# Three one-element vector steps written another way, and rows loaded one tile ahead, in a two-layer mixer kernel

## The chip, the cores and the metric

The kernel runs on one core of a Trainium2 chip. The core has a matrix engine (TensorE, PE in the rows; PEld is its weight load), a vector engine (VectorE, DVE), a scalar engine (ScalarE, ACT), GpSimd (POOL) and SyncE (SP), whose queue issues every DMA of this kernel. Each engine runs its own list of instructions in order and waits for others by semaphores. On-chip memory is SBUF, and PSUM for what the matrix engine writes. The metric is the device time of one execution in microseconds (us).

## The reference

Two layers over a sequence of 1024 rows of width 1024; 16 heads of 64. Layer 0 is a causal attention with a forget gate, layer 1 a sliding-window attention at three dilations.

```python
def rms_norm(x, g):
    xf = x.astype(jnp.float32)
    y = xf * lax.rsqrt(jnp.mean(xf * xf, axis=-1, keepdims=True) + EPS) * g.astype(jnp.float32)
    return y.astype(x.dtype)

def reference(x, positions, norm_g, ...):
    cos, sin = rotary_tables(positions)
    for i in range(DEPTH):                      # DEPTH = 2
        h = rms_norm(x, norm_g[i])
        if i % N_MIXERS == 0:
            o, gate = fox_mixer(h, ...)
        else:
            o, gate = dsw_mixer(h, cos, sin, ...)
        x = x + (o * jax.nn.silu(gate)) @ w_out
    return x
```

The factor 1/sqrt(mean(x²)+eps) of a row is what the change's first part computes. It is needed once for each of the 1024 rows at either layer's input: eight tiles of 128 rows, one row a partition.

## The kernel before

Activations live transposed in SBUF as two parts that sum to the float32 value, `xh` and `xl`, 8 blocks of 128 features by 1024 rows. `project` (L305) multiplies one tile of 128 rows by a slab of weights: for each of the 8 blocks three matmuls (xh·w, xh·w_low, xl·w), 24 in all, into one PSUM tile `pj`. Three `pj` buffers exist; the transposes of `transpose_rows` (`pt`, L322) take theirs from the same three. Where a `pj` has not been read out, the matmuls of a later tile wait.

Weights arrive as `raw` tiles by DMA (`load`, L245, two buffers) and are split into a high part on ScalarE (L286) and a low part on GpSimd or, for some blocks, VectorE (L288).

The program has one order of emission, with a clock of slots (`Flow`): each two blocks of a projection tick it, and work put down for a slot is emitted there. A scheduler of the framework then sets the order of the instructions on VectorE, ScalarE, GpSimd and the DMA queue by its own estimate of durations; TensorE's order is pinned to that of the program.

The change touches two stretches:

- *The first gate part of layer 0 (0 to about 57 us).* `gates` (L463) projects 8 tiles; in front of each, `x_ready` (L570) loads and splits a later tile of x (L525, L528, L530, L531; VectorE or GpSimd multiply and subtract) and calls `row_factor` (L539): a sum of squares on ScalarE (L542), two small steps (L543, L544), `inv_sqrt` (L330 to L336) and a negation (L546). The gate value of tile t takes L475 on VectorE, then L476, L477 and L478 on ScalarE, then L482 on VectorE, which reads `pj` for the last time. `load_gbc` (L359 to L361) and `gain_tables` (L157 to L172) also stand in this stretch.
- *The last part of layer 0's out projection (about 620 to 680 us; `h == 2` in the loop at L761).* For each of 8 tiles: load `xr` (the input rows, three buffers of tag `n2k`) and `xf` (two halves of the rows written by the parts before, seven buffers of tag `ga`), project, add (L780), store (L781), then `norm_rows` (L341): squares on ScalarE (L345), a sum (L347), a scale (L348), `inv_sqrt`, and two products `xn` (L352), stored by L784 and later transposed (L324, copies L327 on ScalarE and L328 on VectorE) into `xh` and `xl`.

`inv_sqrt` takes y = exp(-0.5 ln v) on ScalarE and one Newton step y(1.5 - 0.5 v y²) on VectorE, on tiles of 128 x 1. It is called 8 times in each of the two stretches and nowhere else.

Of the kernel before, what the change touches and what calls it, by code (L numbers as in the profile page):

```python
# [17 lines left out]
ALU = mybir.AluOpType  # L18
# [4 lines left out]
P = 128  # L23
# [3 lines left out]
NT = S // P  # L27
# [24 lines left out]
def tile_cols(g, t):  # L52


    if g < 2:
        return slice(t * P, (t + 1) * P, 1)
    a = 2 * P * (t % 4) + t // 4
    return slice(a, a + 2 * 127 + 1, 2)
# [24 lines left out]
def trunk(ctx, tc, ins, out, cfg):  # L83
    nc = tc.nc
# [31 lines left out]
    def lay(shape, dtype, name, tag):  # L116
        return layer["pool"].tile(shape, dtype, name=name, tag=tag, bufs=layer["bufs"][tag])
# [4 lines left out]
    x1_d = dram.tile([S, D], F32, name="x1_d")  # L122
# [112 lines left out]
    class Weights:  # L235
# [9 lines left out]
        def load(self, i, tag=None):  # L245
            if tag is None:
                self.raw[i] = w_p.tile([P, 2, 384], F32, name="raw", tag="raw", bufs=2)
            else:
                self.raw[i] = lay([P, 2, 384], F32, name="raw", tag=tag)
            nc.sync.dma_start(self.raw[i][:, :, : self.n], self.src[:, 2 * i : 2 * i + 2, :])  # L250
# [51 lines left out]
    def part(src, i, layer=0):  # L302
        return Weights(src[i], src[i].shape[2], None, layer)

    def project(w, cols, last=None):  # L305

        n = w.n
        ps = under["ps"] = ps_pj.tile([P, 512], F32, name="pj", tag="pj")
        for k in range(KT):
            assert k < KT - 2 or last is None or last in turned  # L310
            for i, (a, j) in enumerate(((xh, 0), (xh, 1), (xl, 0))):
                nc.tensor.matmul(ps[:, :n], a[:, k, cols], w.slabs[k][:, j, :n], start=(k == 0 and i == 0), stop=(k == KT - 1 and i == 2))  # L312
            if k % 2:
                flow.tick()
        return ps


    def transpose_half(row, h, t, own=False):
        transpose_rows(row, 4 * h, 4, t, own)
# [10 lines left out]
    def inv_sqrt(y, v, n, a):  # L330

        nc.scalar.activation(y, v, AF.Ln)
        nc.scalar.activation(y, y, AF.Exp, scale=-0.5)
        nc.vector.tensor_mul(a, y, y)
        nc.vector.scalar_tensor_tensor(a, a, -0.5, v, ALU.mult, ALU.mult)
        nc.vector.scalar_tensor_tensor(y, a, 1.5, y, ALU.add, ALU.mult)  # L336

    def rows2(name, tag="ga"):
        return [lay([P, 512], F32, name=f"{name}{h}", tag=tag) for h in range(2)]
# [15 lines left out]
    def load_gbc(layer):  # L355
        gbc = lay([P, D], F32, name="gbc", tag="ph")
        nc.sync.dma_start(gbc, norm_g[layer].partition_broadcast(P))
        gm = gmax[:, layer : layer + 1]
        nc.vector.tensor_reduce(gm, gbc, AX.X, ALU.max, apply_absolute_value=True)  # L359
        nc.vector.tensor_mul(gmax2[:, layer : layer + 1], gm, gm)  # L360
        nc.vector.tensor_scalar(gmax2[:, layer : layer + 1], gmax2[:, layer : layer + 1], 2.0 * D, None, ALU.mult)  # L361
        return gbc
# [365 lines left out]
    for hp in range(NHP):  # L728
# [11 lines left out]
        for t in range(NT):  # L740
# [13 lines left out]
            if hp == NHP - 1:  # L754

                a = max(flow.now + 6, s0 + cfg["due"][t] - 4 * NT + cfg["lpf"] + 9)
# [4 lines left out]
    for h, (c0, n) in enumerate(PARTS):  # L761
        w2 = (part(w_fo, h + 1) if h < 2 else part(w_gate, 0)).ahead()
        if h == 1:
            gbc2 = load_gbc(1)
            rotary_tables()
        for t in range(NT):
            rows = slice(t * P, (t + 1) * P)
            xr = sb.tile([P, n], F32, name="xr", tag="n2k", bufs=cfg["nb"])
            nc.sync.dma_start(xr, x[rows, c0 : c0 + n])
            if h == 2:  # L770
                xf = rows2("xf")
                nc.sync.dma_start(xf[0], x1_d[rows, :512])
                nc.sync.dma_start(xf[1][:, : c0 - 512], x1_d[rows, 512:c0])
            ps = project(w, tile_cols(0, t), t)
            if h < 2:
                xo = sb.tile([P, n], F32, name="xo", tag="n2k", bufs=cfg["nb"])
                nc.vector.tensor_add(xo, ps[:, :n], xr)
                nc.sync.dma_start(x1_d[rows, c0 : c0 + n], xo)
            else:
                nc.vector.tensor_add(xf[1][:, c0 - 512 :], ps[:, :n], xr)  # L780
                nc.sync.dma_start(x1_d[rows, c0:], xf[1][:, c0 - 512 :])  # L781
                xn = norm_rows(xf, gbc2)
                for i in range(2):
                    nc.sync.dma_start(xn_d[rows, i * 512 : (i + 1) * 512], xn[i])  # L784
                    flow.at(flow.now + cfg["lx"] + i, lambda xn=xn, i=i, t=t: transpose_half(xn[i], i, t))
        w = w2
# [185 lines left out]
    for h, (c0, n) in enumerate(PARTS):  # L972
        w2 = part(w_do, h + 1).ahead() if h < 2 else None
        for t in range(NT):
            rows = tile_rows(1, t)
            xr = sb.tile([P, n], F32, name="xr", tag="n2k", bufs=cfg["nb"])
# [59 lines left out]
```

## Time and profile before

| | us |
|---|---|
| time, median of 3 runs | 1816.96 |
| lowest and highest run | 1816.78, 1818.73 |
| the profiled execution | 1819.76 |
| its span, first to last instruction | 1818.0 |
| TensorE busy in the span | 1752.1 (96%) |
| VectorE, ScalarE, GpSimd busy | 1110.1, 985.4, 951.8 |

The profiled execution lies 2.80 us above the median of the timed runs, and 1.76 us of it lie outside the span. The mean granted clock was 0.995 of full speed.

In a row of the timeline the columns are: start in us, duration in us, engine, source line, operation, out<-in by the program's names, shape and type, a count where equal neighbours are merged, and in brackets how long the engine was idle before and what released it. A stretch row of the windows view gives, for each engine, busy us and (x instructions), then the granted clock, the DMA share and GB/s.

### The profile page before, as it was taken

How to read it: one execution, taken by the hardware profiler on the slowest of the kernel's cores; microseconds unless marked ns; L12 is line 12 of the kernel's file. 1: busy time of each engine (PE TensorE's matmuls, PEld its weight loads, DVE VectorE, ACT ScalarE, POOL GpSimd, SP SyncE). 2: the span in 40 equal slices, each digit the busy share in tenths (PEclk: the TensorE clock that was granted, in tenths of full speed). 3: DMA queues.
4: the chain of work that ended last, by engine and by line, in shares of the span. 5: the costliest groups of instructions: out<-in, count | busy, mean ns of one | idle time of the engine just before them, and what ended most of it. 6: DMA issues, size and time to landing. Idle time of an engine off the chain costs nothing.

```text
span 1818.0 us, 39235 instructions
## 1 busy us (share of the span) xinstructions
PE 1752.1 (96%) x13784; PEld 1686.9 (93%) x13784; DVE 1110.1 (61%) x3774; ACT 985.4 (54%) x2642; POOL 951.8 (52%) x1161
## 2 busy tenths in 40 slices
PE   7999999999989989999999999999999999999999
PEld 6999888888878989999999999999999999999899
DVE  8546666766665373365556576676676667767631
ACT  6536666666664354445555665555555555555610
POOL 4215665556653211255656656667576666757520
PEclk9999999999999999999999999999999999999999
DMA  7437999989998563456776696666776766667842
GB/s 287 123 117 137 186 200 184 174 178 183 193 202 198 167 206 113 121 108 140 134 141 144 146 203 132 152 141 152 141 154 151 169 142 142 155 137 189 194 138 93
DMA packets 630790, 289.28 MB, mean 159 GB/s; under 512 B 510384, under 2 KB 595376, under 8 KB 630592
## 3 DMA queue, kind: packets, MB, share of 16 engines
q1 hardware_dynamic: 630592, 286.77, 69.5%
q8 instruction: 108, 1.77, 0.4%
q14 instruction: 90, 0.74, 0.1%
HBM read 124.87 MB, written 37.03 MB: 89 GB/s over the span
## 4 chain that ended last, share of the span: by engine, by line
PE 53%; DMA 17%; DVE 12%; ACT 7%; POOL 5%; issue 4%; SPq 1%; DVEq 0%; POOLq 0%; ACTq 0%
PE pj L312 46%; DMA raw<-in_w_dsw 4%; DMA raw<-in_w_fox 3%; PE s L448 3%; DMA ptt<-ph 3%; POOL w L288 2%; DVE p L659 2%; POOL ph L499 2%; DMA qk_t<-hl 1%; ACT p L493 1%; POOL hl L423 1%; DMA x_d<-xo 1%; ACT ph L496 1%; PE pt L324 1%; ACT w L286 1%
## 5 line engine op out<-in xcount | busy, mean ns | idle before, releaser
L312 PE MATMUL pj<-w,xh 128*128 128x384 f32 (+2 forms) x5632 | 1443.4, 339 | 20.5 <-ACT w L286 6.2
L312 PEld LDWEIGHTS pj<-w,xh 128*128 128x128 f32 x5632 | 999.1, 190 | 30.6 <-ACT w L286 7.3
L312 PE MATMUL pj<-w,xl 128*128 128x384 f32 (+2 forms) x2816 | 939.7, 334 | 4.6 <-DVE xl L328 2.6
L312 PEld LDWEIGHTS pj<-w,xl 128*128 128x128 f32 x2816 | 535.5, 190 | 6.3 <-DVE xl L328 3.3
L288 POOL TENSOR_TENSOR w<-raw,w 128x384 fp32r<-128x384 f32 (+2 forms) x258 | 261.4, 1033 | 305.1 <-ACT w L286 300.1
L499 POOL TENSOR_TENSOR ph<-p,ph 128x512 f16<-128x512 f32 (+3 forms) x176 | 172.7, 998 | 161.5 <-ACT ph L496 138.3
L286 ACT CAST w<-raw 128x384 fp32r<-128x384 f32 (+2 forms) x352 | 162.2, 501 | 120.7 <-PE pj L312 51.9
L423 POOL TENSOR_TENSOR hl<-u,hl 128x512 f16<-128x512 f32 x128 | 150.8, 1178 | 132.0 <-ACT hl L422 132.0
L850 POOL TENSOR_TENSOR ph<-p,ph 128x768 f16<-128x768 f32 (+2 forms) x96 | 155.8, 1623 | 104.8 <-ACT ph L849 104.7
L378 ACT ACTIVATE sq<-pj 128x256 f32<-128x256 f32 x256 | 97.0, 379 | 194.0 <-DVE u L373 192.3
L448 PE MATMUL s<-qk_t 128*128 128x128 f16 (+1 forms) x1504 | 160.9, 247 | 8.5 <-DVE acc L659 6.2
L255 DVE TENSOR_REDUCE vm<-raw 128x1 f32<-128x256 f32 x128 | 53.6, 419 | 156.6 <-DMA raw<-in_w_dsw 111.5
L507 PEld LDWEIGHTS <-ptt 128*128 128x128 f16 x1136 | 103.5, 98 | 43.3 <-issue 24.2
L448 PEld LDWEIGHTS <-qk_t 128*128 128x128 f16 x1504 | 110.6, 98 | 24.6 <-issue 15.4
L493 ACT ACTIVATE p<-p,acc 128x512 f32<-128x512 f32 (+2 forms) x192 | 109.9, 610 | 39.6 <-DVE acc L659 35.5
L422 ACT CAST hl<-u 128x512 f16<-128x512 f32 x128 | 79.1, 618 | 91.4 <-DVE u L420 86.6
L496 ACT CAST ph<-p 128x512 f16<-128x512 f32 (+3 forms) x176 | 89.2, 536 | 60.8 <-DMA ptt<-ph 60.8
L391 DVE TENSOR_REDUCE pj<-sq 128x8 f32<-128x512 f32 x128 | 88.4, 691 | 46.3 <-ACT sq L378 46.2
L845 ACT ACTIVATE p<-p,og 128x128 f32<-128x128 f32 (+1 forms) x256 | 97.8, 441 | 32.6 <-DVE og L844 32.5
L373 DVE TENSOR_TENSOR u<-pj,gr 128x256 f32<-128x256 f32 x256 | 106.4, 416 | 12.4 <-PE pj L312 12.0
L424 DVE COPY hl<-hl 128x512 f16<-128x512 f16 x128 | 61.9, 483 | 78.6 <-POOL hl L423 78.5
L508 PEld LDWEIGHTS <-ptt 128*128 128x128 f16 x1136 | 106.3, 97 | 0.5 <-issue 0.5
(167 smaller groups left out, 2293.2 us busy)
## 6 DMA issues: line engine op xcount, KB each, us to landing
raw<-in_w_dsw SPq DMA_DIRECT2D x96, 384.0 KB, 3.7
raw<-in_w_fox SPq DMA_DIRECT2D x32, 384.0 KB, 3.9
og_d<-og SPq DMA_DIRECT2D x64, 132.0 KB, 2.9
cmb<-og_d SPq DMA_DIRECT2D x64, 132.0 KB, 3.3
bc<-c_d SPq DMA_DIRECT2D x32, 256.0 KB, 3.9
gs_d<-ge SPq DMA_DIRECT2D x32, 192.0 KB, 2.3
xt<-in_xt SPq DMA_DIRECT2D x16, 256.0 KB, 6.1
xrow<-in_x SPq DMA_DIRECT2D x8, 512.0 KB, 6.9
```

Of the source, the lines that this page charges most:

```text
L286: nc.scalar.copy(w[:, 0, :n], raw[:, k % 2, :n])
L288: eng.tensor_sub(w[:, 1, :n], raw[:, k % 2, :n], w[:, 0, :n].bitcast(F32))
L312: nc.tensor.matmul(ps[:, :n], a[:, k, cols], w.slabs[k][:, j, :n], start=(k == 0 and i == 0), stop=(k == KT - 1 and i == 2))
L373: nc.vector.tensor_mul(u[:, t % 2].rearrange("p (a b) d -> p a b d", a=2), ps[:, : 4 * HD].rearrange("p (a b d) -> p a b d", a=2, b=2), gr ...
L423: nc.gpsimd.tensor_sub(hl[:, :, :4, 1], u, hl[:, :, :4, 0])
L448: nc.tensor.matmul(s[:, c0 : c0 + cnt * P].rearrange("p (c s) -> p c s", c=cnt), qk[:, i, blk], kk[:, j : j + cnt, e], start=(h == 0), sto ...
L493: nc.scalar.activation(p, p, AF.Exp, bias=acc, scale=-1.0)
L496: nc.scalar.copy(ph[:, e, 0, cols], p)
L499: (nc.gpsimd if pool_l else nc.vector).tensor_sub(ph[:, e, 1, cols], p, ph[:, e, 0, cols])
L507: nc.tensor.matmul(o[:, e, :], hi, vt[:, j, e, HD:], start=(b == 0), stop=False, skip_group_check=True)
L508: nc.tensor.matmul(o[:, e, :HD], hi, vt[:, j, e, :HD], start=False, stop=False, skip_group_check=True)
L850: nc.gpsimd.tensor_sub(ph[:, 1], st["p"], ph[:, 0])
```

## The change

`inv_sqrt` computes the same Newton step in three instructions that take one tensor and one or two scalars (numbers, or one value a partition) instead of a product of two tensors and two instructions of the form (tensor, scalar, tensor). In the out projection the loads of a tile are put into a function, and in the last part those of tile t+1 are emitted ahead of the projection of tile t.

```diff
         nc.scalar.activation(y, v, AF.Ln)
         nc.scalar.activation(y, y, AF.Exp, scale=-0.5)
-        nc.vector.tensor_mul(a, y, y)
-        nc.vector.scalar_tensor_tensor(a, a, -0.5, v, ALU.mult, ALU.mult)
-        nc.vector.scalar_tensor_tensor(y, a, 1.5, y, ALU.add, ALU.mult)
+        nc.vector.tensor_scalar(a, y, y, -0.5, ALU.mult, ALU.mult)
+        nc.vector.tensor_scalar(a, a, v, 1.5, ALU.mult, ALU.add)
+        nc.vector.tensor_scalar(y, y, a, None, ALU.mult)
...
-        for t in range(NT):
+        def load(t):
             rows = slice(t * P, (t + 1) * P)
             xr = sb.tile([P, n], F32, name="xr", tag="n2k", bufs=cfg["nb"])
             nc.sync.dma_start(xr, x[rows, c0 : c0 + n])
-            if h == 2:
-                xf = rows2("xf")
-                nc.sync.dma_start(xf[0], x1_d[rows, :512])
-                nc.sync.dma_start(xf[1][:, : c0 - 512], x1_d[rows, 512:c0])
+            if h < 2:
+                return xr, None
+            xf = rows2("xf")
+            nc.sync.dma_start(xf[0], x1_d[rows, :512])
+            nc.sync.dma_start(xf[1][:, : c0 - 512], x1_d[rows, 512:c0])
+            return xr, xf
+
+        nxt = None
+        for t in range(NT):
+            rows = slice(t * P, (t + 1) * P)
+
+            xr, xf = nxt or load(t)
+            nxt = load(t + 1) if h == 2 and t + 1 < NT else None
             ps = project(w, tile_cols(0, t), t)
```

The scheduler answers with another order on VectorE, ScalarE and the DMA queue, in these two stretches alone; the orders of TensorE and GpSimd stay as they were. Lines behind the diff count 9 more in the new kernel (L780 becomes L789, L781 L790, L784 L793, L772 L773).

In the first gate part, on VectorE: `pj_216` is tile 0's projection, so L482 on `ge_245` frees its buffer; `nv_264` belongs to tile 2's row factor. Before:

```order
L334 TENSOR_TENSOR nv_264<-rx_123 128x1
L531 TENSOR_TENSOR xl_107<-xt0_252,xh_106 128x4x128
L335 SCALAR_TENSOR_TENSOR nv_264<-nv_264 128x1
L482 SCALAR_TENSOR_TENSOR ge_245<-ge_245,rx_123,pj_216 128x384
L359 TENSOR_REDUCE gmax_115<-gbc_651 128x1
L336 SCALAR_TENSOR_TENSOR rx_123<-nv_264,rx_123 128x1
L183 CAST rt_pf_9212<-rt_pi_9210 128x24
```

The same place in the new kernel:

```order
L334 TENSOR_SCALAR nv_264<-rx_123 128x1
L531 TENSOR_TENSOR xl_107<-xt0_252,xh_106 128x4x128
L335 TENSOR_SCALAR nv_264<-nv_264 128x1
L359 TENSOR_REDUCE gmax_115<-gbc_651 128x1
L183 CAST rt_pf_9212<-rt_pi_9210 128x24
L482 SCALAR_TENSOR_TENSOR ge_245<-ge_245,rx_123,pj_216 128x384
L336 TENSOR_SCALAR rx_123<-rx_123,nv_264 128x1
```

L482 of tile 0 now stands behind the maximum over `gbc` and a small cast.

In the first gate part, on ScalarE: `ge_421` and `ge_477` are the gate values of tiles 3 and 4, `xrow_432` the rows of tile 6. Before:

```order
L476 ACTIVATE ge_421<-ge_421 128x384
L477 ACTIVATE ge_421<-ge_421 128x384
L530 CAST xh_106<-xt0_484 128x4x128
L478 ACTIVATE ge_421<-ge_421 128x384
L476 ACTIVATE ge_477<-ge_477 128x384
L542 ACTIVATE xrow_432,nv_496<-xrow_432 128x1024
```

The same place in the new kernel:

```order
L530 CAST xh_106<-xt0_484 128x4x128
L476 ACTIVATE ge_421<-ge_421 128x384
L542 ACTIVATE xrow_432,nv_496<-xrow_432 128x1024
L476 ACTIVATE ge_477<-ge_477 128x384
L477 ACTIVATE ge_421<-ge_421 128x384
L332 ACTIVATE rx_123<-nv_496 128x1
L477 ACTIVATE ge_477<-ge_477 128x384
L478 ACTIVATE ge_421<-ge_421 128x384
```

Between the first and the last step of tile 3's gate value there now stand the squares of tile 6, two steps of tile 4 and a small step; before, there stood one cast.

In the last part of the out projection, on VectorE, behind the inverse root of tile 0: `xf1_9584` (before) and `xf1_9535` (new) are tile 1's sum. Before:

```order
L336 SCALAR_TENSOR_TENSOR nv_9567<-nv_9567 128x1
L352 SCALAR_TENSOR_TENSOR xn0_9575<-xf0_9528,nv_9567,gbc_9205 128x512
L352 SCALAR_TENSOR_TENSOR xn1_9576<-xf1_9529,nv_9567,gbc_9205 128x512
L780 TENSOR_TENSOR xf1_9584<-pj_9587,xr_9581 128x384
L347 TENSOR_TENSOR nv_9618<-nss_9615 128x1
```

The same place in the new kernel:

```order
L336 TENSOR_SCALAR nv_9573<-nv_9573 128x1
L789 TENSOR_TENSOR xf1_9535<-pj_9593,xr_9532 128x384
L352 SCALAR_TENSOR_TENSOR xn0_9581<-xf0_9528,nv_9573,gbc_9205 128x512
L352 SCALAR_TENSOR_TENSOR xn1_9582<-xf1_9529,nv_9573,gbc_9205 128x512
L347 TENSOR_TENSOR nv_9624<-nss_9621 128x1
```

The sum of tile 1 now stands ahead of tile 0's two products.

On the DMA queue of that part, `xf0_9896` (before) and `xf0_9837` (new) are the rows of tile 6, `xr_9894` and `xr_9835` those of one buffer round. Before:

```order
L784 DMA xn_d_87<-xn0_9683 128x512
L773 DMA xf1_9832<-x1_d_84 128x128
L784 DMA xn_d_87<-xn1_9684 128x512
L772 DMA xf0_9896<-x1_d_84 128x512
L781 DMA x1_d_84<-xf1_9692 128x384
L769 DMA xr_9894<-in_x 128x384
```

The same place in the new kernel:

```order
L793 DMA xn_d_87<-xn0_9689 128x512
L774 DMA xf1_9771<-x1_d_84 128x128
L793 DMA xn_d_87<-xn1_9690 128x512
L790 DMA x1_d_84<-xf1_9641 128x384
L769 DMA xr_9835<-in_x 128x384
L773 DMA xf0_9837<-x1_d_84 128x512
```

The load of tile 6's first half now stands behind a store of tile 3 and a load of `xr`. Of the other loads of this part one moves forward: the second `xr` goes ahead of a `raw` of the next weights.

## Rows read from the trace of the kernel before

**Rows 1.** The head of the page: the span.

```profile
span 1818.0 us, 39235 instructions
```

**Rows 2.** The windows view of four stretches, in this order: the first gate part, the rest of the gate parts and the first head pair, the last two parts of the out projection, the gate parts of layer 1.

```profile
0.00:57.00 57.00, 44.09 (x241) 41.26 (x242) 48.36 (x136) 37.16 (x90) 23.00 (x30) 1.00 0.71 251
57.00:150.00 93.00, 93.00 (x583) 92.21 (x584) 46.92 (x123) 41.47 (x105) 20.59 (x21) 1.00 0.42 119
...
600.00:690.00 90.00, 83.04 (x532) 79.46 (x531) 44.92 (x106) 39.36 (x98) 15.24 (x17) 0.98 0.60 192
690.00:800.00 110.00, 110.00 (x701) 109.51 (x700) 47.14 (x126) 51.67 (x125) 31.35 (x40) 1.00 0.35 101
```

**Rows 3.** TensorE's timeline in the first gate part: five matmuls in front of which the engine stood idle.

```profile
25.57 0.62 PE L312 MATMUL pj<-w,xh 128*128 128x384 f32 x2 [3.01 <-DVE ge L482]
...
29.60 0.44 PE L312 MATMUL pj<-w,xl 128*128 128x384 f32 x1 [1.30 <-DVE xl L531]
...
36.92 0.61 PE L312 MATMUL pj<-w,xh 128*128 128x384 f32 x2 [1.06 <-DVE ge L482]
...
41.56 0.61 PE L312 MATMUL pj<-w,xh 128*128 128x384 f32 x2 [0.18 <-DVE ge L482]
...
56.88 0.52 PE L312 MATMUL pj<-w,xh 128*128 128x272 f32 x2 [0.55 <-DVE ge L482]
```

**Rows 4.** VectorE's timeline in the first gate part: the four long steps of `inv_sqrt`, and L482 of tile 0 with the maximum that changes places with it.

```profile
15.27 0.93 DVE L334 TENSOR_TENSOR nv<-rx 128x1 f32<-128x1 f32 x1
...
16.44 0.46 DVE L336 SCALAR_TENSOR_TENSOR rx<-nv,rx 128x1 f32<-128x1 f32 x1
...
22.77 0.71 DVE L334 TENSOR_TENSOR nv<-rx 128x1 f32<-128x1 f32 x1
...
24.00 0.99 DVE L335 SCALAR_TENSOR_TENSOR nv<-nv 128x1 f32<-128x1 f32 x1
24.92 0.60 DVE L482 SCALAR_TENSOR_TENSOR ge<-ge,rx,pj 128x384 f32<-128x384 f32 x1
25.44 1.21 DVE L359 TENSOR_REDUCE gmax<-gbc 128x1 f32<-128x1024 f32 x1
```

**Rows 5.** GpSimd's timeline in the same stretch.

```profile
15.14 1.05 POOL L525 TENSOR_TENSOR xt<-xt,gt 128x512 f32<-128x512 f32 x1 [12.79 <-DMA xt<-in_xt]
16.26 0.62 POOL L528 CAST xh<-xt 128x512 fp32r<-128x512 f32 x1
...
23.43 1.55 POOL L525 TENSOR_TENSOR xt<-xt,gt 128x512 f32<-128x512 f32 x1
```

**Rows 6.** The view of single source lines over the whole span: duration in ns (min/median/max), first and last start. The L334 row is that of the first gate part; L270 and L739 are other instructions with one tensor and one value a partition.

```profile
L334 DVE TENSOR_TENSOR nv<-rx x8: 147/150/933, 15.3 to 49.7; 128x1 f32<-128x1 f32 x8
...
L335 DVE SCALAR_TENSOR_TENSOR nv<-nv x16: 142/159/991, 16.2 to 672.5; 128x1 f32<-128x1 f32 x16
...
L270 DVE TENSOR_SCALAR v<-v,gmax x32: 203/204/208, 106.5 to 1666.0; 128x1 f32<-128x1 f32 x32
...
L739 DVE TENSOR_SCALAR vsr<-rx,vs x8: 980/1129/1206, 109.4 to 469.4; 128x8 f32<-128x8 f32 x8
```

**Rows 7.** The timeline of all engines at 190 us: one GpSimd instruction and one VectorE instruction inside its time.

```profile
189.59 1.17 POOL L499 TENSOR_TENSOR ph<-p,ph 128x512 f16<-128x512 f32 x1 [4.52 <-ACT ph L496]
...
190.37 0.20 DVE L270 TENSOR_SCALAR v<-v,gmax 128x1 f32<-128x1 f32 x1
```

**Rows 8.** ScalarE's timeline in the first gate part, tile 3's and 4's gate values and the squares of tile 6, then the casts of the weights after next.

```profile
38.23 0.53 ACT L476 ACTIVATE ge<-ge 128x384 f32<-128x384 f32 x1 [2.26 <-DVE ge L475]
...
39.73 0.52 ACT L478 ACTIVATE ge<-ge 128x384 f32<-128x384 f32 x1
40.16 0.51 ACT L476 ACTIVATE ge<-ge 128x384 f32<-128x384 f32 x1
40.57 1.04 ACT L542 ACTIVATE xrow<-xrow 128x1024 f32<-128x1024 f32 x1
...
53.58 0.93 ACT L286 CAST w<-raw 128x384 fp32r<-128x384 f32 x2 [1.28 <-DMA raw<-in_w_fgate]
```

**Rows 9.** The DMA queue's timeline: the two loads of weights that those casts wait for.

```profile
49.84 0.81 SPq L250 DMA_DIRECT2D raw<-in_w_fgate  x2
```

**Rows 10.** TensorE's timeline in the last part of the out projection: four places with idle time in front.

```profile
638.02 0.66 PE L324 MATMUL pt<-ident,xn 128*128 128x128 f32 x4 [1.10 <-DVE xf L780]
...
642.13 1.11 PE L324 MATMUL pt<-ident,xn 128*128 128x128 f32 x4 [2.39 <-DVE xf L780]
...
645.70 0.62 PE L312 MATMUL pj<-w,xh 128*128 128x384 f32 x2 [0.54 <-DVE xl L328]
...
648.30 0.63 PE L324 MATMUL pt<-ident,xn 128*128 128x128 f32 x4 [0.22 <-DVE xl L328]
```

**Rows 11.** VectorE's timeline there: tile 0's products and tile 1's sum.

```profile
636.08 1.41 DVE L352 SCALAR_TENSOR_TENSOR xn<-xf,nv,gbc 128x512 f32<-128x512 f32 x2
637.41 0.55 DVE L780 TENSOR_TENSOR xf<-pj,xr 128x384 f32<-128x384 f32 x1
```

**Rows 12.** The timeline at three places there: the load of tile 4's rows, ScalarE's wait for it, the load of tile 6's rows.

```profile
639.22 0.43 SPq L772 DMA_DIRECT2D xf<-x_d  x1
...
643.12 0.63 ACT L345 ACTIVATE nsq<-xf 128x512 f32<-128x512 f32 x1 [3.55 <-DMA xf<-x_d]
...
648.31 0.37 SPq L772 DMA_DIRECT2D xf<-x_d  x1
```

## The prediction

> **What bounds the kernel now.** I read the windows view first: TensorE is the bound nearly everywhere (57 to 150 us and 690 to 800 us without a gap) [rows 2], so a stall elsewhere counts only where TensorE stands idle. The two stretches that the change touches are such places: TensorE is busy for 44.09 of the first 57 us, while VectorE is busy for 48.36, and for 83.04 of 90 us in the out projection [rows 2]. Then TensorE's timeline says what it waits for. In the first gate part it waits for L482, the last reading of a `pj` buffer, and for L531: 3.01, 1.30, 1.06, 0.18 and 0.55 us [rows 3]. In the out projection it waits for L780 (1.10 and 2.39 us) and for L328 (0.54 and 0.22 us) [rows 10]. Whatever TensorE's start at 56.88 us becomes is carried to the end, since the next 93 us have no idle time to take it up [rows 2].
>
> **The inverse root's steps.** A step of one element normally takes 0.15 or 0.16 us [rows 6]. Four of the 24 in the first gate part are longer: 0.93, 0.46, 0.71 and 0.99 us [rows 4]. Each of them ends with a GpSimd instruction: the first at 16.20 against 16.19, the second at 16.90 against 16.88, the fourth at 24.99 against 24.98 us [rows 4, 5]. So a product of two SBUF tensors on VectorE waits while GpSimd reads SBUF. What they lose is 0.78 + 0.30 + 0.56 + 0.83 = 2.47 us.
>
> Does the new form wait as well? L270 is one: 128 x 1, one tensor and one value a partition. It runs 32 times in 203 to 208 ns [rows 6], once in the middle of a GpSimd instruction [rows 7]. So it doesn't wait, and I take the 2.47 us as gone. But it is not free: 0.204 against 0.15 is 0.05 us more for the value a partition, 24 times in the first gate part, 1.2 us of VectorE; three times in a row, 0.15 us, in each tile of the out projection. L739, the same form on 8 elements, takes 0.98 to 1.21 us, eight times of eight [rows 6]; as I read it, it waits. The size 1 is what protects the new steps.
>
> The Trainium skill has a rule against this change: in "SBUF — State Buffer", section "Who interferes with whom", it says that `tensor_scalar` can enter the modes that take both ports and then contends with GpSimd. The trace agrees for L739 at 1.13 us and disagrees for L270 at 0.204 us; by the rule taken plainly the 2.47 us would stay and the sum would be that of the third rival.
>
> **The first gate part, by what TensorE waits for.** VectorE is nearly full here, and the scheduler orders it anew.
> - 25.57 us, L482 of tile 0. Of the 2.47 us I count 1.5 as won in front of it: behind a step that no longer waits there often stands an L531 or L525 of two tensors, which then waits instead. Eight steps cost 8 x 0.05 = 0.4 us. But the maximum L359 now stands in front of L482: from 25.44 to the next start it took 1.1 us [rows 4], with the cast 1.2 us. Sum -1.5 + 0.4 + 1.2 = +0.1 us: TensorE starts no earlier.
> - 29.60 us: here L359 was paid before as well, so the gain shows: about 0.6 us of the 1.1 (again L531 waits in part). 36.92 us, L482 of tile 2: with the squares of tile 4 earlier on ScalarE I estimate 1.2 us earlier.
> - 41.56 us, L482 of tile 3. It needs L478. Before, ScalarE went from L476 at 38.23 to the end of L478 at 40.25 us, 2.0 us [rows 8]. Now the squares L542 stand between (1.1 us with the reading of the sum), two steps of tile 4 (0.43 us each by the starts 39.73 and 40.16), a small one and then L477 and L478 (0.43 and 0.52): with L476's own 0.43, 3.5 us. L475 of tile 3 I put where it was, since a product and a cast moved in front of it. So L478 ends at about 41.8, L482 at 42.4, and TensorE starts tile 6 0.9 us late. The 1.2 us of the tile before become idle time.
> - 56.88 us. From 41.56 TensorE lost only 0.55 us [rows 3], so 0.9 - 0.55 = 0.35 us are late by its own work. The other chain: L482 of tile 7 stands behind casts that wait for weights until 53.58 [rows 8], loaded at 49.84 [rows 9], when VectorE's L288 had freed the buffer. L288 now stands behind the whole of the gain tables and L475 of tile 6; VectorE carries the 1.2 us of price and waits for ScalarE at tile 3. I put the loads 0.5 us later, and L476 of tile 7, which now stands behind two of the casts, 0.4 us later: together 0.9 us at the most. Value taken: +0.7 us. Bounds: -1.3 (the waits of VectorE go in full and the loads move up) and +2.5 (L288 later by that).
>
> **The out projection.** The load ahead: seven buffers `ga` and three `n2k` already let the queue load two to three tiles ahead, so one `xr` moves in front of a weight load and no `xf` comes earlier by it. What the order gives: tile 1's sum stood behind two products, from 636.08 to 637.41 us [rows 11], and now stands in front. TensorE at 638.02 [rows 10] then waits for the first product, some 0.6 us earlier; at 642.13 the chain of the next tile is 0.75 us earlier. At 645.70 it waits for L328, behind a cast that follows ScalarE's wait for tile 4's rows, until 643.12 [rows 12]; that load goes at 639.22 behind others on SP's queue and moves up by 0.3 us only. With the 0.22 us at 648.30 [rows 10] gone as L328 moves ahead, 0.5 us. Against it: tile 6's rows were loaded at 648.31 [rows 12] and now stand behind tile 3's store and an `xr`, two issues of about 0.45 us and the sum that the store waits for: 1.2 us later. ScalarE squares tile 6's first half ahead of tile 4's second, so the chain of tile 4 is late by some 0.7 us, which 0.5 us of earlier matmuls and the three-buffer slack only just cover. The price of 0.15 us a tile lies on the same chain. Value taken -0.2 us, from -1.2 to +1.0.
>
> **Sum.** +0.7 - 0.2 = +0.5 us on the profiled execution's 1819.76 us (span 1818.0 [rows 1]): 1820.3 us. That execution lies 2.80 us above the median of the timed runs, so the time is 1816.96 + 0.5 = 1817.5 us. Anything within 0.2% (3.6 us) can't be told from no change.
>
> **Rivals.**
> 1. *Faster by more than 0.2%.* VectorE is the first gate part's bound and its wins pass to TensorE in full: the waits of 3.01, 1.30 and 1.06 us go [rows 3], 5.4 us, with 0.5 us in the out projection: 1811.1 us. For it: VectorE's share; against it: L359 in front of L482, and the load at 49.84, in front of which a gain has to come out or be lost. Chance 0.06.
> 2. *Slower by more than 0.2%.* The weights' split L288 behind the gain tables decides: once it frees the `raw` buffer later than 49.84 + 0.35 us, every further us stands at 56.88 as idle time of TensorE, one to one, and is carried to the end. With 24 x 0.05 = 1.2 us of price, the 1.2 us of L359 and 1.5 us of waiting for tile 3's gate value on VectorE the split is 3.9 us late: 1820.9 us. For it: an in-order VectorE with little idle time; against it: 2.47 us of waits gone in front. Chance 0.10.
> 3. *The new steps wait like L739.* Then the 1.5 us that I counted as won are not won: 0.5 + 1.5 = +2.0 us, 1819.0 us. For it stands L739, against it L270 [rows 6, 7]. Chance 0.07, within 0.2%. The page "SBUF — State Buffer" of the Trainium skill, in the section named above, would have it so.
> 4. *The load ahead does not do what it says*: that is in the forecast.
>
> Forecast 0.77. Faster 0.06, the same 0.77 + 0.07 = 0.84, slower 0.10. The range takes the likeliest case with the sum of its bounds, -2.5 to +3.5 us: 1814.5 to 1820.5 us; the rivals outside hold 0.16.
>
> **What would show it.** Right: L334 to L336 at about 0.20 us without an exception in the first gate part; a TensorE start near 25.7 us behind L482, and a wait of some 2.5 us near 42 us behind L482; an idle stretch of TensorE near 57 us; in the out projection tile 1's sum ahead of the products and waits at 638 and 642 us shorter, and the last transposes ending within 1 us of before as seen from 57 us. Wrong: a small step of 0.5 us or more beside a GpSimd instruction; no wait near 42 us; or a difference of more than 2 us that arises between 57 and 600 us, where nothing changes.

## The result, and the profile after

The changed kernel takes 1822.92 us (median of 20, 1817.52 to 1825.54). The kernel before, timed in turn with it, took 1819.26 us here, 2.3 us above its first three runs. The ratio is 1.0020, 95% interval 1.0011 to 1.0030: slower by 3.7 us, between 2.0 and 5.5, where +0.5 was forecast. The profiled execution is the fastest of the 20: 1817.52 us. It is 2.2 us shorter than the profiled execution of the kernel before (1819.76 us), so this pair of profiles can show where work moved, but not the 3.7 us.

The head of its page, and the source view of the new steps (duration in ns as min/median/max, first and last start):

```profile
span 1815.7 us, 39229 instructions
```

```profile
L334 DVE TENSOR_SCALAR nv<-rx x8: 196/200/206, 15.6 to 45.5; 128x1 f32<-128x1 f32 x8
...
L335 DVE TENSOR_SCALAR nv<-nv x16: 199/213/215, 15.8 to 671.9; 128x1 f32<-128x1 f32 x16
```

No step is long any more [rows 4, 6]; each costs the 0.05 us that was put on it.

VectorE's timeline around tile 0's L482, and the three waits of TensorE that answer to [rows 3]. TensorE's first row stands at 6.93 us, 0.73 later than before (6.20), and this is to be taken off:

```profile
24.34 1.20 DVE L359 TENSOR_REDUCE gmax<-gbc 128x1 f32<-128x1024 f32 x1
25.46 0.33 DVE L183 CAST rt_pf<-rt_pi 128x24 f32<-128x24 int32 x1
25.71 0.60 DVE L482 SCALAR_TENSOR_TENSOR ge<-ge,rx,pj 128x384 f32<-128x384 f32 x1
```

```profile
26.36 0.44 PE L312 MATMUL pj<-w,xh 128*128 128x384 f32 x1 [3.81 <-DVE ge L482]
...
42.32 0.44 PE L312 MATMUL pj<-w,xh 128*128 128x384 f32 x1 [1.48 <-DVE ge L482]
...
57.51 0.52 PE L312 MATMUL pj<-w,xh 128*128 128x272 f32 x2 [0.43 <-DVE ge L482]
```

Without the 0.73 us they are 25.63, 41.59 and 56.78 us, within 0.1 us of before. The waits at 29.60 and 36.92 us are gone. But most of the idle time that is left stands in one place: 3.81 us for 3.01. The windows view shows what follows it (columns: stretch, its length, busy time of TensorE, its weight loads, VectorE, ScalarE and GpSimd with counts, the granted clock, DMA share, GB/s). First the kernel before, then after, whose second row is a stretch of the out projection that is read further down:

```profile
24.00:36.00 12.00, 8.98 (x48) 8.34 (x48) 11.70 (x28) 6.42 (x18) 9.57 (x10) 1.00 0.93 329
```

```profile
24.00:36.00 12.00, 9.64 (x46) 9.64 (x47) 11.97 (x30) 6.67 (x18) 7.60 (x9) 0.86 0.97 350
640.00:654.00 14.00, 10.74 (x57) 10.25 (x56) 8.20 (x22) 7.50 (x22) 0.00 (x0) 0.88 0.62 215
```

A granted clock of 0.86 over 12 us is 1.68 us of full-speed work not done: part of the stretch stood at 1.2 instead of 2.4 GHz. I call this a piece. In all profiles of this study the low clock comes in pieces of about this size, some 1.7 us of work each, at times two in a row.

Near 50 us the two loads of weights [rows 9] drift apart. SyncE's and ScalarE's timeline:

```profile
49.54 2.30 SPq L250 DMA_DIRECT2D raw<-in_w_fgate  x2
```

```profile
49.06 0.53 ACT L476 ACTIVATE ge<-ge 128x384 f32<-128x384 f32 x1 [0.75 <-DVE ge L475]
49.49 0.40 ACT L286 CAST w<-raw 128x272 fp32r<-128x272 f32 x1
...
50.23 0.40 ACT L286 CAST w<-raw 128x272 fp32r<-128x272 f32 x1
...
55.46 0.93 ACT L286 CAST w<-raw 128x384 fp32r<-128x384 f32 x2 [0.82 <-DMA raw<-in_w_fgate]
```

Before, both were issued within 0.81 us. Now the second waits until the casts behind tile 6's L476 have freed its buffer.

In the out projection the last part begins at 618.16 us and its last transposes at 681.74: 63.58 us for 61.47 before (620.92 to 682.39). TensorE's timeline, ScalarE's, VectorE's and SyncE's:

```profile
638.91 0.66 PE L324 MATMUL pt<-ident,xn 128*128 128x128 f32 x4 [2.35 <-DVE xf L789]
...
643.88 0.62 PE L312 MATMUL pj<-w,xh 128*128 128x384 f32 x2 [3.25 <-DVE xl L328]
...
645.90 0.84 PE L312 MATMUL pj<-w,xh 128*128 128x384 f32 x2
```

```profile
641.29 0.63 ACT L345 ACTIVATE nsq<-xf 128x512 f32<-128x512 f32 x1 [5.10 <-DMA xf<-x_d]
...
642.53 0.56 ACT L327 CAST xh<-pt 128x512 fp32r<-128x512 f32 x1
```

```profile
643.13 0.69 DVE L328 TENSOR_TENSOR xl<-pt,xh 128x512 fp32r<-128x512 f32 x1
```

```profile
635.02 1.03 SPq L793 DMA_DIRECT2D xn_d<-xn  x2
636.09 0.45 SPq L774 DMA_DIRECT2D xf<-x_d  x1
636.58 0.97 SPq L773 DMA_DIRECT2D xf<-x_d  x1
```

The wait at 638.02 [rows 10] is down from 1.10 to 0.17 us, but the one ahead of tile 4's products grew from 0.54 to 3.25. Its PSUM bank is freed by L328, behind a cast (L327) that stands on ScalarE behind the square of tile 4's rows (L345), and these rows land late. The pair of products at 645.90 takes 0.84 us for 0.51: the low clock again.

### The profile page after: what moved, and what is told of

It is laid out like the page before. It is cut to its first block, busy times and chain, and to the rows that moved or that the text cites. A ratio compares the mean times of both kernels' runs of the same rounds, so it can differ in the third digit from the quotient of the medians.

```text
span 1815.7 us, 39229 instructions
## 1 busy us (share of the span) xinstructions
PE 1750.5 (96%) x13784; PEld 1687.6 (93%) x13784; DVE 1102.9 (61%) x3774; ACT 985.2 (54%) x2642; POOL 951.1 (52%) x1161
## 4 chain that ended last, share of the span: by engine, by line
PE 54%; DMA 16%; DVE 10%; POOL 6%; ACT 6%; issue 6%; SPq 1%; POOLq 0%; DVEq 0%; ACTq 0%
PE pj L312 46%; DMA raw<-in_w_dsw 4%; PE s L448 3%; DMA ptt<-ph 3%; POOL w L288 3%; DMA raw<-in_w_fox 2%; POOL ph L499 2%; DVE p L659 1%; PE pt L324 1%; DMA x_d<-xo 1%; POOL hl L423 1%; ACT p L493 1%; ACT ph L496 1%; DMA og_d<-og 1%; DMA qk_t<-hl 1%
## 5 line engine op out<-in xcount | busy, mean ns | idle before, releaser
L288 POOL TENSOR_TENSOR w<-raw,w 128x384 fp32r<-128x384 f32 (+2 forms) x258 | 261.2, 1032 | 305.9 <-ACT w L286 285.0
```

Of the source, the lines that this page charges most:

```text
L288: eng.tensor_sub(w[:, 1, :n], raw[:, k % 2, :n], w[:, 0, :n].bitcast(F32))
```

## The experiments

Eighteen kernels beside the kernel before. The table has one line for each. *Ratio*: to the kernel before on the same chip in turn. *Clock*: mean granted clock over all timed executions, this / before; 0.001 of 1816 us is 1.8 us. The other columns are of one profile each: *start*, attention's first product minus TensorE's first row; *part*, length of the out projection's last part as above; *pieces* at the low clock, up to 66 us and in the last part. Single profiles scatter: from attention's first product to the start of that last part, where no instruction differs, these twenty take 471.8 to 480.2 us, and behind the last transposes 1125.9 to 1138.1 us.

| run | ratio, 95% | clock | start us | pieces | part us | pieces |
|---|---|---|---|---|---|---|
| before | | | 134.5 | 0 | 61.5 | 1 |
| after | 1.0020 (1.0011–1.0030) | 0.9926 | 134.4 | 1 | 63.6 | 1 |
| e1 after again | 1.0026 (1.0013–1.0038) | 0.9923 / 0.9944 | 136.9 | 2 | 63.6 | 2 |
| e2 null | 1.0001 (0.9990–1.0013) | 0.9937 / 0.9944 | 134.4 | 1 | 60.4 | 0 |
| e3 steps alone | 0.9991 (0.9977–1.0005) | 0.9950 / 0.9944 | 136.4 | 1 | 60.9 | 0 |
| e4 load alone | 1.0014 (1.0002–1.0027) | 0.9940 / 0.9944 | 135.3 | 1 | 61.2 | 1 |
| e5 more buffers | 1.0009 (0.9995–1.0022) | 0.9936 / 0.9941 | 136.2 | 2 | 63.3 | 1 |
| e6 same, no load ahead | 1.0021 (1.0008–1.0034) | 0.9928 / 0.9941 | 134.1 | 1 | 63.6 | 2 |
| e7 stores by GpSimd | 1.0013 (1.0002–1.0024) | 0.9937 / 0.9941 | 137.3 | 3 | 59.2 | 0 |
| e8 wait filled | 1.0005 (0.9995–1.0015) | 0.9933 / 0.9941 | 134.9 | 1 | 64.0 | 1 |
| e9 gate part only | 1.0011 (1.0000–1.0023) | 0.9932 / 0.9942 | 136.3 | 2 | 63.7 | 2 |
| e10 out projection only | 1.0007 (0.9994–1.0020) | 0.9935 / 0.9942 | 134.8 | 1 | 63.5 | 1 |
| e11 steps alone again | 1.0011 (1.0000–1.0023) | 0.9938 / 0.9942 | 138.0 | 3 | 62.0 | 1 |
| e12 before, GpSimd stores | 1.0000 (0.9985–1.0015) | 0.9952 / 0.9942 | 134.1 | 0 | 59.5 | 0 |
| e13 casts on VectorE | 1.0010 (0.9998–1.0021) | 0.9928 / 0.9945 | 138.4 | 2 | 59.5 | 1 |
| e14 both repairs | 1.0014 (1.0004–1.0024) | 0.9928 / 0.9945 | 138.0 | 3 | 58.8 | 0 |
| e15 repairs, no load ahead | 0.9997 (0.9987–1.0007) | 0.9933 / 0.9945 | 135.5 | 2 | 58.7 | 1 |
| e16 filled again | 0.9995 (0.9986–1.0004) | 0.9943 / 0.9945 | 136.5 | 1 | 63.8 | 0 |
| e17 gate wait filled | 0.9971 (0.9958–0.9984) | 0.9949 / 0.9941 | 136.6 | 1 | 63.0 | 2 |
| e18 both waits filled | 0.9934 (0.9922–0.9947) | 0.9982 / 0.9941 | 135.4 | 1 | 63.9 | 1 |

**The change taken apart.** e1 is the changed kernel unaltered; e2 has both edits undone in its text; e3 keeps `nxt = None`; e4 keeps the old three steps. The theories are numbered in e1's expectation.

> The changed kernel once more, unaltered, beside the kernel before. Theory 1 (the loads of layer 1's out projection): from the start of its last part to its last transpose some 63.6 us as in the first profile of the changed kernel (61.5 in the kernel before), with one wait of TensorE above 3 us near the middle of the part, and the whole some 2 us, a thousandth, above the kernel before. Theory 2 (the first gate part): its end, taken from TensorE's first row, at least 1 us later than the 50.7 us of the kernel before. Theory 3 (the scalar read through a pointer costs 0.05 us in each of 32 steps on the path): spread over both places, at most 1.6 us. Theory 4 (scatter between executions): a ratio between 0.999 and 1.001.

> The changed kernel's text with both edits undone (the old three steps, no load ahead), so the instructions of the kernel before in the same order on each engine. All theories: a ratio of 1.000 within 0.0005; a last part of the out projection of 61.5 us. If it differs by more than 0.001, the scatter between builds is as large as what is to be explained, and theory 4 holds.

> The new inverse root's steps without the load ahead. In the first gate part this is the changed kernel's order; in the out projection the stores and loads of SyncE's queue stand in yet another order (the second half of tile 4's rows is asked for behind the next rows of x, the sums ahead of the stores of the normed rows). Theory 1: the order of SyncE's queue makes the loss, so this kernel loses too, about 1 to 2 us (1.0005 to 1.001), if the load of tile 4's first half lands later than 22.2 us behind the start of the part, and nothing if it doesn't. Theory 2: all of the loss is here, 1.001 to 1.002, with the first gate part over 1 us longer. Theory 3: 1.0005 to 1.001 with no single long wait. Theory 4: 1.000.

> The load ahead with the old three steps. The first gate part is that of the kernel before. Theory 1: the loss depends on how SyncE's queue falls out; in this kernel the two stores of tile 0's normed rows stand as before, and tile 4's first half is asked for ahead of the stores of tile 1, so at most 1 us (1.0000 to 1.0005). Theories 2 and 3: 1.000, the last part of the out projection as before. Theory 4: 1.000.

The loss is there again (1.0026), and the null stands at 1.0001. The scatter of executions, some 3 us to either side, is what makes intervals of 0.12%. e4 missed: 1.0014, where every theory had at most 1.0005. e3 stands below 1 with the price of 0.05 us paid in full, but its repeat e11 (below) gives 1.0011. So neither theory 3 nor the share of each edit is settled by these runs.

**Four repairs of the last part.** e5 and e6 take six more buffers, e6 without the load ahead; e7 changes the queue of the stores; e8 puts products into TensorE's wait.

```
e5, e6:  xf = rows2("xf", "qk_t" if t % 2 else "ga")
e7:      nc.gpsimd.dma_start(xn_d[rows, ...], xn[i])
e8:      if h == 2 and t == 4:
             dm = ps_o.tile([P, 512], F32, name="dm", tag="o")
             for i in range(16):
                 nc.tensor.matmul(dm[:, :n], xh[:, 0, tile_cols(0, 0)], w.slabs[0][:, 0, :n], start=True, stop=True)
```

> The changed kernel, but the rows of the odd tiles of the last part go into buffers that layer 1's attention has left (six more), so that the rows of tiles 4 to 6 are asked for before the part begins and wait for no buffer of tile 0. Theory 1 (TensorE waits at the start of tile 4's products because ScalarE's square of tile 4's rows, which stands ahead of the cast that frees a PSUM bank, waits for a load that is issued late): the wait of 3.3 to 3.5 us at 24.5 to 25.7 us goes to under 1 us, and with it the rows at the low clock; the part takes 60 to 61.5 us for 63.6, and the ratio falls from 1.0026 to about 1.001 or below. Theory 4 (scatter, or something outside of the part): the part as short, but the ratio stays above 1.002.

> The same six buffers, the new steps, but no load ahead. Theory 1: the load ahead was never needed, since the first half of a row waits for a buffer and for nothing else: part of 60 to 61.5 us, as with the load ahead in this form; the ratio 0.998 to 1.000. A rival, that the load ahead is worth something once buffers are there: at least 0.5 us longer in the part than the run with both.

> The changed kernel, but the stores of the normed rows are issued by GpSimd's queue, so that none stands ahead of a load on SyncE's. Orders of TensorE, VectorE and ScalarE are the changed kernel's up to tile 0's transposes. Theory 1 in the form that the two stores ahead of the load of tile 4's first half delay it: that load is issued 1 us earlier and lands 1 us earlier (22 us behind the start of the part for 23.1), the wait of TensorE falls from 3.3 to 2.3 us or less, and the part takes 61.5 to 62.5 us. Rival form, that the load waits for the buffer of tile 0 or for the transfer itself, and the stores in front cost nothing: it lands at 22.7 us or later and the part stays at 63 us or more.

> The changed kernel with 16 products more, of 128x384, ahead of those of tile 4 in the last part, into a PSUM bank that nothing reads: 2.8 us of TensorE work at 0.176 us each, inside the wait of 3.3 to 3.5 us. What is left of theory 1 is tested by it: if the granted clock falls after the wait because TensorE stood idle, the rows behind it stay at 0.51 us a pair (0.84 in the changed kernel), the start of tile 4's products doesn't move, and the part is 0.8 to 1.3 us shorter (62.3 to 62.8 us). If the clock has another cause, the rows at 0.84 us stay, and the part stays at 63.6 us or is longer by up to 2.8 us.

e5 moved the loss: the wait at tile 4 fell to 1.30 us, but the earlier loads hold up the weights, TensorE waits 3.12 us for L288 at the part's start, and the part stays at 63.3. e6 missed as well (63.6); there the part itself begins behind a wait of 2.93 us. e8 was built wrongly: its products read the columns that tile 0's transposes write, so they waited 2.48 us themselves. In e8, as later in e16 and e18, the scheduler also gave VectorE, ScalarE and the DMA queue another order behind the filling, so the filling is not the only difference in the rest of the part.

e7 does what theory 1 says of the queue. SyncE's timeline and TensorE's; the part begins at 623.62 us:

```profile
639.39 0.43 SPq L774 DMA_DIRECT2D xf<-x_d  x1
639.93 0.36 SPq L773 DMA_DIRECT2D xf<-x_d  x1
```

```profile
646.95 0.62 PE L312 MATMUL pj<-w,xh 128*128 128x384 f32 x2 [1.96 <-DVE xl L328]
```

Tile 4's load goes at 16.3 us behind the part's start (18.4 in the changed kernel), ScalarE squares at 20.75 (23.13), the part is 59.2 us. Still the ratio is 1.0013: in this profile three pieces at the low clock stand ahead of 66 us. So the first gate part had to be looked at.

**The change taken apart by place.** e9 has the new steps in the first gate part alone, e10 in the out projection alone, with the load ahead. e9's out projection and e10's gate part are in every engine's order those of the kernel before.

> The new steps in the first gate part alone; the out projection is the kernel before's, instruction by instruction, and the first gate part the changed kernel's. So far the 57 us mark (TensorE's wait for VectorE near the end of the first gate part) stood at 56.9 to 57.7 us in three profiles with the old steps and at 57.5 to 60.3 us in six with the new. Theory 2, in the form that the gate part is one half of the loss: a mark at 58 us or later, and 1.0005 to 1.0015. Theory 1 alone: a mark below 57.7 us and 1.000.

> The other half: the first gate part is the kernel before's, the out projection the changed kernel's (new steps in the norm, load ahead). Theory 1: a wait of TensorE above 3 us at tile 4's products, the part at 63 to 64 us, and from the out projection's first sum to the last transpose 145 to 147 us (142 to 143.5 in the kernel before); the ratio 1.0010 to 1.0020. Theory 2 alone: 1.000, the part at 61.5 us.

> The run with the new steps and no load ahead once more, since its first time (0.9991) doesn't fit the marks of its own profile (first gate part 2 to 3 us later, out projection 1.5 us longer than the kernel before). If the marks tell the truth: 1.0005 to 1.0015. If the first time does: 0.9985 to 0.9995, and marks of single profiles are no measure of the gate part.

> A candidate for a faster kernel: both edits undone, and the stores of the normed rows issued by GpSimd, so that no load on SyncE's queue stands behind them. Theory 1 (the loads' place in the queue sets the waits of the last part): the part 59 to 60.5 us (61.5 and 60.4 before), 0.9985 to 0.9995. If the part's time is set elsewhere: 1.000, or above where the stores hold up GpSimd's halves of the weights.

The two ratios add up, 1.0011 and 1.0007 to 1.0018 for 1.0020 and 1.0026, but both intervals reach 1.0000, so it is not shown by them that each place has its half. In e10 the wait at tile 4 was 2.50 us, where theory 1 had above 3. By the profiles, with e9's first gate part and e10's:

```profile
24.00:36.00 12.00, 9.87 (x43) 9.87 (x44) 11.97 (x30) 6.70 (x17) 6.90 (x8) 0.72 0.95 351
```

```profile
24.00:36.00 12.00, 10.09 (x48) 9.69 (x48) 11.71 (x29) 6.49 (x17) 9.36 (x9) 0.86 0.89 318
```

Two pieces (0.72) and one. Over all profiles with the old gate part (before, e2, e4, e10, e12) TensorE's wait near 26 us is 3.01 or 3.02 us, a piece follows in 3 of 5, and attention starts 134.6 us behind the first row on average. With the new order, before any filling, the wait is 3.69 to 3.82 us, a piece follows it in 13 of 13, and often a second or one behind the wait near 59 us; in the ten of them whose gate part is otherwise as in the changed kernel, 1.7 pieces on average (0.6 with the old order), and attention at 136.1 us: +1.5 us. In this stretch TensorE stands idle for 6.6 us on average with the new order and for 5.7 with the old. e11 is e3 once more: 1.0011 for 0.9991, together 1.0001. Two measurements of one kernel thus differ by 0.0020, outside of each other's interval and as much as the loss itself, so a single ratio is less sure here than its interval says. e12 shortens the part to 59.5 us and the time not at all (1.0000).

In the last part the three profiles of the old order (before, e2, e9) have 61.5, 60.4 and 63.7 us, of the changed one (after, e1, e10) 63.6, 63.6 and 63.5: +1.7 us. With e13 below, whose last part is in the old order too (59.5), and e17 in the changed one (63.0), it is +2.2; but one profile of the old order, e9, is as long as the changed ones. The square of tile 4's rows starts 22.2, 20.7 and 22.8 us behind the part's start against 23.1, 22.0 and 23.8. From the issue of the load to that square it takes 3.5 to 3.9 us in the old order and 4.7 to 5.2 in the new, where two stores and the other half row stand right in front of it. That the stores are the reason is not shown: in e7 and e14, where GpSimd issues them, it still takes 4.4 and 4.9 us, and what these two gain is an earlier issue (16.3 and 15.5 us behind the part's start).

**Repairs and fillings.** e13 to e15 take two casts from ScalarE; e14 is the changed kernel with this and with e7's stores, e15 the same without the load ahead and with the old steps in the norm. e16 is e8 with `tile_cols(0, NT - 1)`, columns that are written much later.

```
e13 to e15, in split():
    if n == 272 and k >= KT - 2:
        nc.vector.tensor_copy(w[:, 0, :n], raw[:, k % 2, :n])
    else:
        nc.scalar.copy(w[:, 0, :n], raw[:, k % 2, :n])
```

> New steps in the first gate part, out projection of the kernel before, and the last two casts of the 272 columns wide weights on VectorE instead of ScalarE. If those two casts behind tile 6's activations are what the gate part loses by: the two weight loads near 50 us are issued within 0.9 us of each other (1.8 to 2.4 us with the new steps so far), TensorE's wait near 59 us is under 0.6 us (mean 1.1 in nine profiles), attention begins 134 to 135 us behind TensorE's first row (136.1 on average with the new steps, 134.6 with the old), and the ratio falls from 1.0011 to 0.9995 to 1.0005. If not: 136 us and 1.001.

> The changed kernel, steps and load ahead, with both repairs: two casts on VectorE, the stores of the normed rows issued by GpSimd. If the two places are the whole loss: 0.9990 to 1.0005 for 1.0020 and 1.0026, the last part at 59 to 60 us, attention 134 to 135 us behind the first row. If there is a third cause: still 1.001 or more.

> The version that should beat both kernels if the reasons hold: new steps in the first gate part, no load ahead, old steps in the norm, two casts on VectorE, stores of the normed rows by GpSimd. Expected 0.9980 to 0.9995, the last part at 59 to 60 us. The stores by GpSimd alone gave 1.0000; so if nothing is to be had here it is 1.000.

> The filling of TensorE's wait once more, with the 16 products now from columns that no transpose of the part has written yet, so that they can start at once. If idleness lowers the clock: pairs behind the wait at 0.51 us, tile 4's products begin where they began (24.5 to 25.7 us), and the part is 62.3 to 62.8 us. If the clock falls for another reason: pairs at 0.84 us behind the filling, and 63.6 us or more.

e13 missed: on VectorE the casts stand behind the gain tables, and issuing the two loads still takes 2.03 us. So ScalarE's place alone isn't what holds up the buffer; VectorE's tables in front of tile 6's L475 may be, but a kernel with the tables moved wasn't run. e14 has a part of 58.8 us and keeps a ratio of 1.0014; its gate part is as late as ever, with three pieces up to 66 us and attention at 138.0. e15 missed with 0.9997, for 0.9980 to 0.9995.

e16 kept the clock at 1.00 through the last part:

```profile
641.33 2.98 PE L786 MATMUL dm<-w,xh 128*128 128x384 f32 x16
...
645.02 0.62 PE L312 MATMUL pj<-w,xh 128*128 128x384 f32 x2 [0.71 <-DVE xl L328]
...
651.92 0.59 PE L312 MATMUL pj<-w,xh 128*128 128x384 f32 x2 [1.53 <-DVE xl L328]
```

Tile 1's second transposes come at 28.5 us behind the part's start (31.0 in the changed kernel), and the next wait takes the 2.4 us back: tile 2's come at 34.4 for 34.6. So within the part the rows set the end and the clock is hidden (63.8 us, where 62.3 to 62.8 was expected); yet over eleven executions the kernel stands at 0.9995.

The last two fill the gate part's wait, alone and with e16's filling. No other engine's order changes in e17.

```
e17, in gates(), ahead of tile 3's products:
    if h == 0 and rows is not None and t == 3:
        dg = ps_o.tile([P, 512], F32, name="dg", tag="o")
        for i in range(18):
            nc.tensor.matmul(dg[:, :384], xh[:, 0, tile_cols(0, 0)], w.slabs[0][:, 0, :384], start=True, stop=True)
```

> The changed kernel with 18 products more, of 128x384, into a PSUM bank that nothing reads, in TensorE's wait of 3.8 us in the first gate part (3.2 us of work at 0.176 us each); all other engines' orders are unchanged. If the low clock behind the wait is half of the loss: no piece at the low clock between 24 and 36 us, mean granted clock of all executions 0.9933 to 0.9940 for 0.9923 to 0.9926, attention 134 to 135.3 us behind TensorE's first row for 136.1, the ratio 1.0005 to 1.0015 for 1.0020 to 1.0026. If it's the data that is late: the clock rises, and the ratio stays at 1.002.

> Both waits filled, the one in the first gate part and the one ahead of tile 4's products in the out projection's last part (its filling alone gave 0.9995). If the clock is the loss: mean granted clock 0.9945 to 0.9955, ratio 0.9980 to 0.9992, so a version of the changed kernel that is faster than the kernel before. If only the out projection's filling counts: 0.9995 as with that alone.

TensorE's timeline of e17 and the windows of e18:

```profile
23.73 3.33 PE L473 MATMUL dg<-w,xh 128*128 128x384 f32 x18
27.70 0.62 PE L312 MATMUL pj<-w,xh 128*128 128x384 f32 x2 [0.64 <-DVE ge L486]
43.65 0.62 PE L312 MATMUL pj<-w,xh 128*128 128x384 f32 x2 [2.93 <-DVE ge L486]
```

```profile
24.00:36.00 12.00, 11.37 (x64) 10.90 (x63) 11.97 (x30) 7.52 (x20) 9.01 (x9) 1.00 1.00 374
36.00:48.00 12.00, 9.78 (x47) 9.46 (x47) 11.05 (x51) 7.06 (x18) 0.99 (x1) 0.86 0.24 83
```

No piece follows the filled wait in either. But part of the idle time moves on to 43 us, where a piece follows a wait of 2.93 us (2.22 us in e18). So attention starts no earlier: 136.6 us in e17, where 134 to 135.3 was expected, and 135.4 in e18, together 136.0 for 136.1 without the filling. e18's last part takes 63.9 us.

Both kernels are faster than the kernel before by more than any forecast: 0.9971, and 0.9934 with five executions between 1805.03 and 1810.02 us against fifteen between 1814.16 and 1824.10. The clock rose to 0.9982 in e18, by 0.0041, worth 7.4 us of the 12, and by 0.0008 in e17, worth 1.5 of 5.3. The profiles do not put this gain where the fillings stand. e18's is 9.8 us shorter than that of the kernel before, yet TensorE's first row is 0.9 us later, and the stretch from there to attention is 0.8 us longer, the last part 2.5. It is shorter where no instruction differs: by 5.1 us between attention and the last part, with one piece at the low clock there for four, and by 8.9 us behind the last transposes (1126.7 us for 1135.6; 1125.9 in e16). Small waits make up the latter, and they scatter between executions. Part of it may be that the kernel before was 1819.8 us in this series and 1810.3 in the one before it, on the same chip; against 1810.3, e17 (1813.60 us) stands at 1.0018 and e18 (1807.62) at 0.9985. That the fillings made the kernel faster is not shown.

## Why the prediction was wrong

- **The price and the gain of the steps: right.** 0.20 us forecast, 0.196 to 0.216 measured; no long step is left, so the third rival falls. The rule of the Trainium skill weighed there ("SBUF — State Buffer", section "Who interferes with whom"), that `tensor_scalar` can contend with GpSimd, did not come true for one element: 13 of the 24 steps of the first gate part ran while a GpSimd instruction did, and none took more than 0.215 us.
- **25.57 us, "+0.1: TensorE starts no earlier": right, and here is a step that failed.** The start is 25.63 on the old scale. But TensorE comes there earlier, because the small waits in front are gone, and stands idle for 3.8 instead of 3.0 us. The forecast summed idle times by where they end and had no term for the clock behind a longer one. Where it had +0.7, the gate part took +1.5 us on average, with 0.9 us more of idle time and 1.7 pieces for 0.6. That idleness brings the low clock is shown by e17 and e18, which change nothing in the gate part but what TensorE does in this wait: the piece behind it is gone in both, and there in 13 of 13 profiles without the filling. The Trainium skill's page "TensorE: Matmul & The Clock Gate", section "HAM oscillation — how this bites in real kernels", describes waits for data that put the array back to half rate time after time; these 13 profiles agree. How much of the +1.5 us is the clock's is not shown: with the piece gone, attention started as late as without the filling (136.0 us on average), so the cause of this size stays open.
- **Near 42 us: half right.** A wait for L482 of tile 3 came (1.48 us for 2.5), the 0.9 us of delay did not: 41.59 for 41.56.
- **56.88 us.** The forecast put the loads 0.5 us later. The first was on time; issuing the two takes 1.8 to 2.4 us in every profile with the new order and 0.8 with the old. The second rival named the mechanism (the split behind the gain tables frees `raw` late), but TensorE's wait there grew from 0.4 to 1.1 us on average, not by 3.4. That its +3.9 us is close to the measured 3.7 is luck.
- **The out projection, -0.2: wrong by 1.9 us in the profiles.** Tile 1's sum ahead of the products did shorten the first wait, not the one at 642 us (2.35 us for 2.39). The failed step is "that load moves up by 0.3 us only": it is issued 0.2 us earlier on average, but its rows are there, and the square starts, some 1 us later; the forecast had no term for a longer way from issue to landing. Why it grew is not shown. The wait at tile 4, taken as 0.5 us shorter, became the longest of the part (3.25 us for 0.54).
- **Rival 4** held as to the order, in which the load ahead moves one `xr` and no `xf`; alone (e4) it measured 1.0014, with the interval down to 1.0002.
- **A sign that misled.** A difference of more than 2 us between 57 and 600 us was to show the forecast wrong. From attention's first product to the last part the changed kernel's profile is 3.4 us shorter, but with a scatter of 8 us there this says nothing.

Sum by the profiles: +1.5 and +1.7 to +2.2 are 3.2 to 3.7 us; measured 3.7 (2.0 to 5.5). With a few profiles each, and more scatter than that outside of the two stretches, so close a fit is in part luck. Of the 5.4 us between 1817.5 and 1822.92, 2.3 are the kernel before's own, which was slower in the comparison than in its first three runs.

## What to carry to other kernels

Don't only add up what an engine waits; look at how long it stands idle in one piece. In the first pair of profiles here TensorE's idle time up to attention fell from 6.7 to 6.0 us, but more of what was left stood in one place, and the clock fell behind it. Products into a bank that nothing reads kept the clock up over such a wait (e16 to e18). They did not make the filled stretch shorter, since the rows behind it were late in any case; the gain that e17 and e18 show as whole kernels is not explained. A load that is moved in a queue is to be priced by when it lands, not by when it is issued. And where a loss is as small as this one, measure one kernel twice: e3 and e11 differ by as much.

## What the runs showed of the hardware

- The low clock came in pieces that cost some 1.7 us of work each. In or behind waits of 3.0 us near 26 us a piece followed in 3 of 5 profiles, with 3.7 to 3.8 us in 13 of 13; elsewhere it also followed shorter ones (1.75 us in e5, 2.22 in e18, 2.93 in e17).
- Mean granted clock goes with the time, but loosely: 0.9923 in e1 at +4.7 us, 0.9952 in e12 at 0, 0.9949 in e17 at -5.3, 0.9982 in e18 at -12 us. Over e1 to e16 the ratio's correlation with the difference of the clocks is -0.66, with the sum of the columns start and part 0.35.
- A step of one element with one tensor and one value a partition ran beside GpSimd in 0.196 to 0.215 us. The same form on 8 elements (L739, in the kernel before) took 0.98 to 1.21 us, and a GpSimd instruction ended within 0.04 us before it in 8 of 8.
- The same first loads of the program, issued at the same moments (within 0.02 us), let TensorE start between 5.97 and 7.42 us.
